# Issuing the low halves of weights one pair later, behind the next pair's sums and high halves

## The chip, the cores and the metric

The kernel runs on one core of a Trainium2 chip. Its engines work side by side, each through a queue of its own, in the order of the program: TensorE (PE) multiplies, VectorE (DVE) and ScalarE (ACT) work element by element, GpSimd (POOL) does a little, SyncE (SP) issues the transfers from the chip's memory. They wait for one another through semaphores. The metric is the time of one execution on the device, in microseconds (us); lower is better.

## The reference

The kernel computes one block of a streaming encoder on x of 256 positions by 2048 features, in fp32:

```python
x = x + 0.5 * swiglu(rms_norm(x), w_gate_1, w_up_1, w_down_1)
h = rms_norm(x);  P = h @ W_in
m = sigmoid(gate_gdn) * (gated_delta_net(P) @ W_A) + sigmoid(gate_att) * (chunk_attention(P) @ W_B)
x = x + m @ W_out
x = x + 0.5 * swiglu(rms_norm(x), w_gate_2, w_up_2, w_down_2)

def swiglu(h, w_gate, w_up, w_down):
    return (silu(h @ w_gate) * (h @ w_up)) @ w_down
```

The hidden width of the two feed-forward stages is 5504. Their weights, and those of the projections of the mixing stage between them, are read once from memory, and nearly all of the time goes into multiplying by them.

## The kernel before

**Numbers in two halves.** A product of fp32 accuracy is made of three matmuls on TensorE's fp32r format. Each operand is written as a high half (the value rounded to fp32r) and a low half (the value less its high half). `product` issues high by high (L359), high by low (L360) and low by high (L361) into one PSUM bank; the second operand is the weight.

**Weights come in pairs.** `plan` lists all weights in the order of use. `load` fetches one pair, two transfers of 512 KB on SP's queue (L283), into a raw buffer of 128x2x1024. `prepare` makes the halves. For a plain pair it does so piece by piece: ScalarE casts the high half (L113), VectorE subtracts it from the raw weight for the low half (L114), both 128x1024. Before it prepares a pair it sees that two more are loaded (LOAD = 2). `take_weights` hands the next weights out and prepares until more than PREP = 5 units stand ready (a piece is one unit, a fast pair four).

**Plain and fast pairs.** The gate and up products of a feed-forward stage run over 11 groups of 512 hidden columns (the last has 384), and in each group over 8 pairs j of 256 input features, with the gate weight and the up weight in one pair. Pairs 0, 2 and 5 (FAST) are fast, except in group 0 of the first stage: instead of 8 block products they use 7, on sums of blocks, in the manner of Winograd's scheme. That needs 24 matmuls for a plain pair and 21 for a fast one, 183 in a group. For a fast pair `prepare_sums` has VectorE make four sums S1 to S4 of weight blocks (L317 for two, L318, L319), has ScalarE cast the highs of the blocks that are used as they are (w and v, L325) and of the four sums (sh, 128x2048), and has VectorE subtract for the lows (L327), the last of them sl, 128x2048.

**A group.** `gate_up` goes through the 8 pairs and adds each product to one of 8 PSUM banks: four from the pool acc (results 1 to 4) and four from core (5 to 8). After the last fast pair it moves the banks of the fast products into four tiles e (L426 to L430). At the end of the group VectorE adds the four remaining banks, 2, 3, 4 and 8 (L439), ScalarE applies SiLU (L443), and VectorE multiplies gate by up (L446). A group's result is transposed on TensorE and split into halves (hid) a few pairs into the next group. Groups form chunks of 4, 4 and 3; behind each chunk the down product (pd) uses its hidden columns.

**The start.** In group 0 of the first stage, `feed(j)` brings x in: it scales and splits the block of x for pair j + 1 (L157, L158), issues the transfer of another block (L74), and from pair 3 on transposes x for the norm (`stand`). `finish` then takes the square root for the norm's factor rn, which the SiLU of the group needs.

**What sets the order.** Each engine's queue is the program's order as the scheduler lays it out from the order in which the Python code issues instructions. An instruction that waits holds everything behind it on its engine. The buffers of weights, their halves and the activations come from one heap of 22 slots.

**The mixing stage** multiplies by projections in the same way (pgt is one of its results). Near its middle GpSimd clears buffers (L818, L823) and copies blocks into them (L825, L826), which a small matmul of TensorE (pd, L858) waits for.

Of the kernel before, what the change touches and what calls it, by code (L numbers as in the profile page):

```python
# [12 lines left out]
F32R = mybir.dt.float32r  # L13
# [22 lines left out]
def block_kernel(ctx: ExitStack, tc: tile.TileContext, a: dict, out: bass.AP):  # L36
# [248 lines left out]
                nc.sync.dma_start(raw[:, at, : n * kk], src)  # L285
        loaded.append((i, fast, pieces, raw))

    def prepare():

        while len(loaded) < 1 + LOAD and len(loaded) < left[0]:  # L290
            load()
        left[0] -= 1
        i, fast, pieces, raw = loaded.popleft()
        if fast:
            return prepare_sums(i, pieces[0][1] * P, raw)
        for at, (src, n, kk) in enumerate(pieces):
            m = n * kk * (P if len(src.shape) == 3 else 1)
            w = heap([P, 2, 1024], F32R, f"w{i}{at}")
            hi, lo = w[:, 0, :m], w[:, 1, :m]
            split_to(hi, lo, raw[:, at, :m])  # L300
            if len(src.shape) == 3:
                n *= P
                cols = lambda w: [w.rearrange("p (c k x) -> p c k x", k=kk, x=P)[:, :, j, :] for j in range(kk)]
            else:
                cols = lambda w: [w[:, j * n : (j + 1) * n] for j in range(kk)]
            ready.append((1, (cols(hi), cols(lo), n)))

    def prepare_sums(i, n, raw):

        s = heap([P, 4, n], F32, f"s{i}")  # L310
        sh, sl = (heap([P, 4, n], F32R, f"s{x}{i}") for x in "hl")
        w1 = heap([P, 2, 2 * n], F32R, f"w{i}")
        w2 = heap([P, 2, n], F32R, f"v{i}")
        R = raw[:, :, : 2 * n].rearrange("p b (c k x) -> p b c k x", k=2, x=P)
        S = s.rearrange("p b (c x) -> p b c x", x=P)
        for b in range(2):
            nc.vector.tensor_sub(S[:, b], R[:, 1, :, b], R[:, b, :, 0])  # L317
        nc.vector.tensor_add(S[:, 2], S[:, 1], R[:, 0, :, 0])  # L318
        nc.vector.tensor_sub(S[:, 3], R[:, 0, :, 1], S[:, 2])  # L319
        col = lambda w: w.rearrange("p (c x) -> p c x", x=P)  # L320
        parts = (
            (w1[:, 0], w1[:, 1], raw[:, 0, : 2 * n]), (col(w2[:, 0]), col(w2[:, 1]), R[:, 1, :, 1]), (sh, sl, s),
        )
        for hi, lo, src in parts:
            nc.scalar.copy(hi, src)  # L325
        for hi, lo, src in parts:
            nc.vector.tensor_sub(lo, src, f32(hi))  # L327
        k = w1.rearrange("p s (c k x) -> p s c k x", k=2, x=P)
        w11, w21 = ([k[:, s, :, b, :] for s in range(2)] for b in range(2))
        t1, t3, t2, t4 = ((sh[:, b], sl[:, b]) for b in range(4))  # L330
        w22 = (w2[:, 0], w2[:, 1])

        ready.append((4, ((1, 0, w11), (2, 2, w21), (6, 5, t2), (7, 6, t3), (4, 3, t4), (5, 4, t1), (3, 7, w22))))

    left = [sum(1 for _ in plan())]

    def take_weights():
        tick()
        while sum(c for c, _ in ready) <= PREP and left[0]:
            prepare()  # L340
        return ready.popleft()[1]

    def run(gen):
# [42 lines left out]
    def gate_up(nm, f, i, xr, jobs, feed):  # L386
# [16 lines left out]
        ev = {}  # L403
        idle = 0
        for j in range(KD // 2):
            if feed:
                feed(j)
            if j in fast:
                ps = take_weights()
                for at, (b, i7, w) in enumerate(ps):  # L410
# [3 lines left out]
            else:  # L414
                for s in range(2):
                    wh, wl, _ = take_weights()
                    for k, w in enumerate(zip(wh, wl)):
                        for t in range(2):
                            add((2, 4, 3, 8)[2 * s + t], xr.st(2 * j + k, t), w)
                    idle += 1  # L420
                    if idle > 3 and jobs:
                        jobs.popleft()()
# [751 lines left out]
```

## Time and profile before

| | |
|---|---|
| median of 3 runs | 2180.31 us (2178.92 to 2181.02) |
| the profiled execution | 2180.59 us |
| its span, first to last instruction | 2178.8 us |
| TensorE busy | 2140.7 us, 98% of the span |
| VectorE busy | 1521.9 us, 70% |
| ScalarE busy | 1087.6 us, 50% |
| memory traffic | 434.61 MB, mean 199 GB/s |
| mean granted clock of TensorE | 0.998 of full speed |

The page's own share of the chain of work that ended last is PE 89%, DVE 5%, ACT 3%, issue 1%, DMA 1%. Busy time says how long an engine had work, not that the work was dense: matmuls overlap, one is recorded as 0.39 us long while the next starts 0.23 us after it. Where TensorE loses time is read from the distance of starts and from the waits, not from the busy share.

### The profile page before, as it was taken

The page shows a single profiled execution, that of the slowest core. Times are in us where ns is not written, and L with a number is a line of the kernel's source. Part 1 is how long each engine was busy: PE and PEld are TensorE (multiplying, and loading weights), DVE is VectorE, ACT ScalarE, POOL GpSimd, SP SyncE. Part 2 cuts the span into 40 slices and gives each one's busy share as a digit, 9 for nine tenths or more (in the row PEclk, how much of TensorE's full clock was granted, in tenths as well). Part 3 has the DMA queues.
Part 4 walks back from the last instruction along what each step waited for, and adds up shares of the span by engine and source line. Part 5 has one row for each costly group of instructions (what it writes and reads, how often), then busy time and mean ns, then how long its engine had stood idle before and what let it go on. Part 6 is the DMA issues. An engine that isn't in the chain of part 4 may idle for free.

```text
span 2178.8 us, 26078 instructions
## 1 busy us (share of the span) xinstructions
PE 2140.7 (98%) x9902; PEld 1776.1 (82%) x9902; DVE 1521.9 (70%) x1895; ACT 1087.6 (50%) x1318; POOL 8.3 (0%) x13
## 2 busy tenths in 40 slices
PE   7999999999999999999999999999999999999999
PEld 6777888788888988888878888887778887788887
DVE  6788587885867654666875645658886768857683
ACT  6555354553535544467645643545454435544351
POOL 0000000000000000000010000000000000000000
PEclk9999999999999999999999999999999999999999
DMA  9557765577647665445454556666568655686482
GB/s 302 190 179 226 241 208 181 182 239 234 213 146 252 247 215 195 156 134 176 160 174 155 176 191 201 197 210 199 189 192 255 222 191 174 205 258 214 155 265 83
DMA packets 397150, 434.61 MB, mean 199 GB/s; under 512 B 14672, under 2 KB 371296, under 8 KB 396768
## 3 DMA queue, kind: packets, MB, share of 16 engines
q1 hardware_dynamic: 397024, 432.95, 61.2%
q8 instruction: 77, 1.26, 0.2%
q14 instruction: 49, 0.40, 0.1%
HBM read 416.11 MB, written 16.79 MB: 199 GB/s over the span
## 4 chain that ended last, share of the span: by engine, by line
PE 89%; DVE 5%; ACT 3%; issue 1%; DMA 1%; POOL 0%; SPq 0%; ACTq 0%; DVEq 0%
PE pf L360 13%; PE pf L361 12%; PE pf L359 11%; PE pd L361 7%; PE pd L359 7%; PE pd L360 7%; DVE w L114 2%; PE pc L359 2%; PE pc L361 2%; PE pc L360 2%; PE pgt L359 2%; PE pgt L361 2%; PE pgt L360 2%; ACT w L113 2%; PE pwo L361 1%; PE pwo L360 1%
## 5 line engine op out<-in xcount | busy, mean ns | idle before, releaser
L114 DVE TENSOR_TENSOR w<-raw,w 128x1024 fp32r<-128x1024 f32 (+3 forms) x648 | 752.6, 1195 | 243.9 <-ACT w L113 239.4
L113 ACT CAST w<-raw 128x1024 fp32r<-128x1024 f32 (+3 forms) x648 | 640.4, 1031 | 292.4 <-PE pd L361 116.6
L359 PE MATMUL pf<-w,xr 128*128 128x512 f32 (+1 forms) x880 | 336.4, 388 | 5.7 <-ACT w L113 5.7
L360 PE MATMUL pf<-w,xr 128*128 128x512 f32 (+1 forms) x880 | 340.1, 386 | 1.9 <-DVE w L114 1.0
L361 PE MATMUL pf<-w,xr 128*128 128x512 f32 (+1 forms) x880 | 338.4, 385 | 0.0
L359 PE MATMUL pd<-w,hid 128*128 128x512 f32 x688 | 269.6, 392 | 0.0
L360 PE MATMUL pd<-w,hid 128*128 128x512 f32 x688 | 268.5, 390 | 0.0
L361 PE MATMUL pd<-w,hid 128*128 128x512 f32 x688 | 268.2, 390 | 0.0
L325 ACT CAST sh<-s 128x2048 fp32r<-128x2048 f32 (+1 forms) x63 | 117.7, 1868 | 265.9 <-DVE s L319 265.9
L327 DVE TENSOR_TENSOR sl<-s,sh 128x2048 fp32r<-128x2048 f32 (+1 forms) x63 | 141.1, 2239 | 88.0 <-ACT sh L325 88.0
L359 PEld LDWEIGHTS pf<-w,xr 128*128 128x128 f32 x880 | 164.1, 188 | 43.9 <-ACT w L113 13.9
L360 PEld LDWEIGHTS pf<-w,xr 128*128 128x128 f32 x880 | 165.3, 188 | 38.4 <-DVE w L114 7.6
L361 PEld LDWEIGHTS pf<-w,xr 128*128 128x128 f32 x880 | 165.3, 188 | 30.7
L361 PEld LDWEIGHTS pd<-w,hid 128*128 128x128 f32 x688 | 129.2, 188 | 26.7
L359 PEld LDWEIGHTS pd<-w,hid 128*128 128x128 f32 x688 | 129.2, 188 | 26.6
L360 PEld LDWEIGHTS pd<-w,hid 128*128 128x128 f32 x688 | 129.3, 188 | 26.4
L359 PE MATMUL pgt<-w,xr 128*128 128x512 f32 x256 | 102.0, 398 | 0.0
L360 PE MATMUL pf<-sl,xf 128*128 128x512 f32 (+1 forms) x252 | 99.3, 395 | 2.4 <-DVE sl L327 2.4
L361 PE MATMUL pgt<-w,xr 128*128 128x512 f32 x256 | 100.8, 394 | 0.0
L360 PE MATMUL pgt<-w,xr 128*128 128x512 f32 x256 | 100.6, 393 | 0.0
L361 PE MATMUL pf<-sh,xf 128*128 128x512 f32 (+1 forms) x252 | 97.0, 387 | 0.0
L359 PE MATMUL pf<-sh,xf 128*128 128x512 f32 (+1 forms) x252 | 88.7, 396 | 5.3 <-ACT sh L325 5.3
(324 smaller groups left out, 3214.8 us busy)
## 6 DMA issues: line engine op xcount, KB each, us to landing
raw<-wd SPq DMA_DIRECT2D x168, 512.0 KB, 5.1
raw<-wg SPq DMA_DIRECT2D x160, 512.0 KB, 3.7
raw<-wu SPq DMA_DIRECT2D x160, 512.0 KB, 4.8
raw<-wgt SPq DMA_DIRECT2D x64, 512.0 KB, 4.6
raw<-wa SPq DMA_DIRECT2D x48, 512.0 KB, 4.6
raw<-wc SPq DMA_DIRECT2D x48, 512.0 KB, 4.2
raw<-wbr SPq DMA_DIRECT2D x32, 512.0 KB, 4.4
raw<-wo SPq DMA_DIRECT2D x32, 512.0 KB, 5.9
```

What stands on the lines that cost most here:

```text
L113: nc.scalar.copy(hi, src)
L114: nc.vector.tensor_sub(lo, src, f32(hi))
L325: nc.scalar.copy(hi, src)
L327: nc.vector.tensor_sub(lo, src, f32(hi))
L359: nc.tensor.matmul(dst, ah, wh, start=start, stop=False)
L360: nc.tensor.matmul(dst, ah, wl, start=False, stop=False)
L361: nc.tensor.matmul(dst, al, wh, start=False, stop=stop)
```

## The change

`prepare_sums` and the old `prepare` become one function `begin` for the first part of a pair: the loads behind it, the sums (two of the four now in one operation of 128x1024), and all casts of high halves. What is left to do, the subtractions for low halves, goes on a list with the weights (`begun`). `prepare` then issues a pair's lows only after the next pair's `begin`. At the very first `take_weights` nothing stands ready, no next pair is begun, and the loop stops as soon as one pair is prepared (min(PREP, taken[0])). `feed(j)` is called behind the first `take_weights` of the pair and no longer ahead of it.

```diff
--- before.py
+++ after.py
@@ -285,59 +285,75 @@
                 nc.sync.dma_start(raw[:, at, : n * kk], src)
         loaded.append((i, fast, pieces, raw))
 
-    def prepare():
+    def begin():
+
 
         while len(loaded) < 1 + LOAD and len(loaded) < left[0]:
             load()
         left[0] -= 1
         i, fast, pieces, raw = loaded.popleft()
-        if fast:
-            return prepare_sums(i, pieces[0][1] * P, raw)
-        for at, (src, n, kk) in enumerate(pieces):
-            m = n * kk * (P if len(src.shape) == 3 else 1)
-            w = heap([P, 2, 1024], F32R, f"w{i}{at}")
-            hi, lo = w[:, 0, :m], w[:, 1, :m]
-            split_to(hi, lo, raw[:, at, :m])
-            if len(src.shape) == 3:
-                n *= P
-                cols = lambda w: [w.rearrange("p (c k x) -> p c k x", k=kk, x=P)[:, :, j, :] for j in range(kk)]
-            else:
-                cols = lambda w: [w[:, j * n : (j + 1) * n] for j in range(kk)]
-            ready.append((1, (cols(hi), cols(lo), n)))
-
-    def prepare_sums(i, n, raw):
-
+        if not fast:
+            todo, out = [], []
+            for at, (src, n, kk) in enumerate(pieces):
+                m = n * kk * (P if len(src.shape) == 3 else 1)
+                w = heap([P, 2, 1024], F32R, f"w{i}{at}")
+                hi, lo = w[:, 0, :m], w[:, 1, :m]
+                nc.scalar.copy(hi, raw[:, at, :m])
+                todo.append((hi, lo, raw[:, at, :m]))
+                if len(src.shape) == 3:
+                    n *= P
+                    cols = [w[:, s, :m].rearrange("p (c k x) -> p c k x", k=kk, x=P) for s in range(2)]
+                    cols = [[w[:, :, j, :] for j in range(kk)] for w in cols]
+                else:
+                    cols = [[w[:, s, j * n : (j + 1) * n] for j in range(kk)] for s in range(2)]
+                out.append((1, (*cols, n)))
+            begun.append((todo, out))
+            return
+        n = pieces[0][1] * P
         s = heap([P, 4, n], F32, f"s{i}")
-        sh, sl = (heap([P, 4, n], F32R, f"s{x}{i}") for x in "hl")
         w1 = heap([P, 2, 2 * n], F32R, f"w{i}")
         w2 = heap([P, 2, n], F32R, f"v{i}")
         R = raw[:, :, : 2 * n].rearrange("p b (c k x) -> p b c k x", k=2, x=P)
         S = s.rearrange("p b (c x) -> p b c x", x=P)
-        for b in range(2):
-            nc.vector.tensor_sub(S[:, b], R[:, 1, :, b], R[:, b, :, 0])
+        nc.vector.tensor_sub(S[:, 0:2], R[:, 1].rearrange("p c k x -> p k c x"), R[:, :, :, 0])
         nc.vector.tensor_add(S[:, 2], S[:, 1], R[:, 0, :, 0])
         nc.vector.tensor_sub(S[:, 3], R[:, 0, :, 1], S[:, 2])
         col = lambda w: w.rearrange("p (c x) -> p c x", x=P)
-        parts = (
-            (w1[:, 0], w1[:, 1], raw[:, 0, : 2 * n]), (col(w2[:, 0]), col(w2[:, 1]), R[:, 1, :, 1]), (sh, sl, s),
-        )
+        parts = [(w1[:, 0], w1[:, 1], raw[:, 0, : 2 * n]), (col(w2[:, 0]), col(w2[:, 1]), R[:, 1, :, 1])]
         for hi, lo, src in parts:
             nc.scalar.copy(hi, src)
-        for hi, lo, src in parts:
-            nc.vector.tensor_sub(lo, src, f32(hi))
+        sh, sl = (heap([P, 4, n], F32R, f"s{x}{i}") for x in "hl")
+        nc.scalar.copy(sh, s)
+        parts.append((sh, sl, s))
         k = w1.rearrange("p s (c k x) -> p s c k x", k=2, x=P)
         w11, w21 = ([k[:, s, :, b, :] for s in range(2)] for b in range(2))
         t1, t3, t2, t4 = ((sh[:, b], sl[:, b]) for b in range(4))
         w22 = (w2[:, 0], w2[:, 1])
 
-        ready.append((4, ((1, 0, w11), (2, 2, w21), (6, 5, t2), (7, 6, t3), (4, 3, t4), (5, 4, t1), (3, 7, w22))))
+        prods = ((1, 0, w11), (2, 2, w21), (6, 5, t2), (7, 6, t3), (4, 3, t4), (5, 4, t1), (3, 7, w22))
+        begun.append((parts, [(4, prods)]))
+
+    begun = deque()
+    taken = [0]
+
+    def prepare():
+
+        if not begun or (taken[0] and left[0]):
+            begin()
+        if len(begun) == 1 and taken[0] and left[0]:
+            begin()
+        todo, out = begun.popleft()
+        for hi, lo, src in todo:
+            nc.vector.tensor_sub(lo, src, f32(hi))
+        ready.extend(out)
 
     left = [sum(1 for _ in plan())]
 
     def take_weights():
         tick()
-        while sum(c for c, _ in ready) <= PREP and left[0]:
+        while sum(c for c, _ in ready) <= min(PREP, taken[0]) and (left[0] or begun):
             prepare()
+        taken[0] += 1
         return ready.popleft()[1]
 
     def run(gen):
@@ -403,8 +419,6 @@
         ev = {}
         idle = 0
         for j in range(KD // 2):
-            if feed:
-                feed(j)
             if j in fast:
                 ps = take_weights()
                 for at, (b, i7, w) in enumerate(ps):
@@ -414,6 +428,8 @@
             else:
                 for s in range(2):
                     wh, wl, _ = take_weights()
+                    if feed and s == 0:
+                        feed(j)
                     for k, w in enumerate(zip(wh, wl)):
                         for t in range(2):
                             add((2, 4, 3, 8)[2 * s + t], xr.st(2 * j + k, t), w)
```

The scheduler turns this into another order on each engine. ScalarE at the start, from its first scaling of x on (raw_95 and raw_98 are the first two pairs' raw buffers, xf_0 and xr_1 the blocks of x for pairs 0 and 1):

```order
L157 ACTIVATE xf_0_102<-xT_80,vec 128x256 x2
L157 ACTIVATE xr_1_109<-xT_80,vec 128x256 x2
L113 CAST w_118<-raw_95 128x1024
L113 CAST w_121<-raw_95 128x1024
L157 ACTIVATE xr_1_109<-xT_80,vec 128x256 x2
L113 CAST w_127<-raw_98 128x1024
L113 CAST w_130<-raw_98 128x1024
```

The same place in the changed kernel:

```order
L157 ACTIVATE xf_0_102<-xT_80,vec 128x256 x2
L301 CAST w_112<-raw_95 128x1024
L301 CAST w_114<-raw_95 128x1024
L157 ACTIVATE xr_1_118<-xT_80,vec 128x256 x2
L301 CAST w_141<-raw_98 128x1024
L301 CAST w_143<-raw_98 128x1024
L301 CAST w_148<-raw_109 128x1024
```

The cast of the first weights now stands ahead of the scaling of the second block of x.

SyncE's queue at the same place (raw_98 is the second raw pair, xT are blocks of x). Before:

```order
L283 DMA raw_98<-wg 128x4x256
L283 DMA raw_98<-wu 128x4x256
L74 DMA xT_80<-x 128x512 x3
L1005 DMA cst<-cst 128x768
L283 DMA raw_115<-wg 128x4x256
L283 DMA raw_115<-wu 128x4x256
L283 DMA raw_124<-wg 128x4x256
L283 DMA raw_124<-wu 128x4x256
```

And in the changed kernel, right behind the second raw pair:

```order
L74 DMA xT_80<-x 128x512
L283 DMA raw_109<-wg 128x4x256
L283 DMA raw_109<-wu 128x4x256
L74 DMA xT_80<-x 128x512
L283 DMA raw_138<-wg 128x4x256
L283 DMA raw_138<-wu 128x4x256
L283 DMA raw_145<-wg 128x4x256
L283 DMA raw_145<-wu 128x4x256
L283 DMA raw_168<-wg 128x4x256
L283 DMA raw_168<-wu 128x4x256
L74 DMA xT_80<-x 128x512
L1021 DMA cst<-cst 128x768
```

Before, three transfers of x and the constants stand between the second raw pair (raw_98) and the third (raw_115). Now one transfer of x stands there, another behind the third raw pair, and the third, with the constants, behind the sixth (raw_168).

VectorE where the third group of the first stage begins (names with 4 in e_4 belong to the second group; sl_818 and sl_820 are the low sums of the third group's fast pair 0). Before:

```order
L317 TENSOR_TENSOR s_816<-raw_753 128x512 x2
L327 TENSOR_TENSOR w_819<-raw_753,w_819 128x1024
L318 TENSOR_TENSOR s_816<-s_816,raw_753 128x512
L327 TENSOR_TENSOR v_820<-raw_753,v_820 128x512
L319 TENSOR_TENSOR s_816<-raw_753,s_816 128x512
L439 TENSOR_TENSOR e_4_0_795<-pf_4_2_579,e_4_0_795 128x512
L439 TENSOR_TENSOR e_4_1_796<-pf_4_3_599,e_4_1_796 128x512
L439 TENSOR_TENSOR e_4_2_797<-pf_4_4_591,e_4_2_797 128x512
L439 TENSOR_TENSOR e_4_3_798<-pf_4_8_645,e_4_3_798 128x512
L327 TENSOR_TENSOR sl_818<-s_816,sh_817 128x2048
L114 TENSOR_TENSOR w_870<-raw_804,w_870 128x1024
L114 TENSOR_TENSOR w_873<-raw_804,w_873 128x1024
```

And in the changed kernel:

```order
L320 TENSOR_TENSOR s_811<-raw_697,s_811 128x512
L347 TENSOR_TENSOR v_813<-raw_697,v_813 128x512
L455 TENSOR_TENSOR e_4_0_799<-pf_4_2_592,e_4_0_799 128x512
L455 TENSOR_TENSOR e_4_2_801<-pf_4_4_604,e_4_2_801 128x512
L347 TENSOR_TENSOR sl_820<-s_811,sh_819 128x2048
L318 TENSOR_TENSOR s_873<-raw_808 128x1024
L347 TENSOR_TENSOR w_827<-raw_757,w_827 128x1024
L319 TENSOR_TENSOR s_873<-s_873,raw_808 128x512
L347 TENSOR_TENSOR w_829<-raw_757,w_829 128x1024
L320 TENSOR_TENSOR s_873<-raw_808,s_873 128x512
L455 TENSOR_TENSOR e_4_1_800<-pf_4_3_612,e_4_1_800 128x512
L455 TENSOR_TENSOR e_4_3_802<-pf_4_8_650,e_4_3_802 128x512
```

Before, all four additions of banks stand ahead of the low sums. Now the additions of banks 2 and 4 do, and those of 3 and 8 stand behind the low sums, behind the next fast pair's four sums (s_873) and the two lows of the plain pair between (w_827, w_829).

TensorE in that same fast pair 0, from the sixth of its matmuls on (sh and sl are the halves of the sums, w and v those of the blocks used as they are; line numbers of the changed kernel are 16 higher). Before:

```order
L361 MATMUL pf_8_2_901<-w_819,xf_0_102 128x512
L359 MATMUL pf_8_6_905<-sh_817,xf_0_102 128x512
L359 MATMUL pf_8_7_909<-sh_817,xf_0_102 128x512
L359 MATMUL pf_8_4_913<-sh_817,xf_0_102 128x512
L359 MATMUL pf_8_5_917<-sh_817,xf_0_102 128x512
L359 MATMUL pf_8_3_921<-v_820,xf_0_102 128x512
L360 MATMUL pf_8_3_921<-v_820,xf_0_102 128x512
L361 MATMUL pf_8_3_921<-v_820,xf_0_102 128x512
L359 MATMUL pf_8_2_901<-w_870,xr_1_109 128x512
L360 MATMUL pf_8_6_905<-sl_818,xf_0_102 128x512
L361 MATMUL pf_8_6_905<-sh_817,xf_0_102 128x512
L360 MATMUL pf_8_7_909<-sl_818,xf_0_102 128x512
```

And in the changed kernel:

```order
L377 MATMUL pf_8_2_911<-w_812,xf_0_102 128x512
L375 MATMUL pf_8_6_915<-sh_819,xf_0_102 128x512
L376 MATMUL pf_8_6_915<-sl_820,xf_0_102 128x512
L377 MATMUL pf_8_6_915<-sh_819,xf_0_102 128x512
L375 MATMUL pf_8_7_919<-sh_819,xf_0_102 128x512
L376 MATMUL pf_8_7_919<-sl_820,xf_0_102 128x512
L377 MATMUL pf_8_7_919<-sh_819,xf_0_102 128x512
L375 MATMUL pf_8_4_923<-sh_819,xf_0_102 128x512
L376 MATMUL pf_8_4_923<-sl_820,xf_0_102 128x512
```

The high sums are first used by the 7th matmul of the pair in both kernels. The low sums were first used by the 15th, and now are by the 8th.

## Rows read from the trace of the kernel before

**Rows 1.** The page, part 1: busy time of each engine over the span.
```profile
PE 2140.7 (98%) x9902; PEld 1776.1 (82%) x9902; DVE 1521.9 (70%) x1895; ACT 1087.6 (50%) x1318; POOL 8.3 (0%) x13
```

**Rows 2.** The view of waits, TensorE only: tile and line that waited, engine, tile and line waited for; us in total, times, longest.
```profile
PE pf L359 <- ACT w L113: 19.9, 14, 14.2
PE pf L359 <- ACT sh L325: 5.3, 11, 1.1
PE pd L858 <- POOL gdn_pk L826: 2.7, 1, 2.7
PE pf L360 <- DVE sl L327: 2.4, 9, 0.8
PE pf L359 <- ACT g L443: 1.2, 1, 1.2
PE pf L360 <- DVE w L114: 1.0, 6, 0.2
```

**Rows 3.** Windows from the first use of a fast pair's low sums to the same place one group later, in a chunk of each of the two feed-forward stages; columns: window, length, then busy time (instructions) of PE, PEld, DVE, ACT, POOL, granted TensorE clock, DMA share, GB/s.
```profile
113.15:158.22 45.07, 43.94 (x192) 34.72 (x192) 38.34 (x44) 22.46 (x25) 0.00 (x0) 1.00 0.58 187
...
1815.18:1860.23 45.05, 44.07 (x191) 34.64 (x191) 38.34 (x44) 22.48 (x25) 0.00 (x0) 1.00 0.58 187
```

**Rows 4.** The timeline of TensorE in the first of these groups; columns: start, length, engine, line, operation, output<-inputs, shape, count, and in brackets the idle time before and its releaser.
```profile
115.34 0.39 PE L361 MATMUL pf<-w,xr 128*128 128x512 f32 x1
...
120.10 0.39 PE L361 MATMUL pf<-w,xr 128*128 128x512 f32 x1
...
122.14 0.39 PE L361 MATMUL pf<-v,xf 128*128 128x512 f32 x1
122.89 1.20 PE L359 MATMUL pf<-sh,xf 128*128 128x512 f32 x4 [0.36 <-ACT sh L325]
...
124.78 0.73 PE L359 MATMUL pf<-w,xr 128*128 128x512 f32 x2 [0.45 <-ACT w L113]
125.35 0.39 PE L360 MATMUL pf<-sl,xf 128*128 128x512 f32 x1
...
140.13 0.39 PE L359 MATMUL pf<-sh,xf 128*128 128x512 f32 x1
...
142.09 0.40 PE L360 MATMUL pf<-sl,xf 128*128 128x512 f32 x1
```

**Rows 5.** The timeline of VectorE and ScalarE around the first two fast pairs of that group (pair 0 starts on TensorE at 109.49, pair 2 at 120.33).
```profile
109.01 1.89 DVE L439 TENSOR_TENSOR e<-pf,e 128x512 f32<-128x512 f32 x3 [0.20 <-PE pf L361]
110.82 2.28 DVE L327 TENSOR_TENSOR sl<-s,sh 128x2048 fp32r<-128x2048 f32 x1
...
120.93 1.91 ACT L325 CAST sh<-s 128x2048 fp32r<-128x2048 f32 x1 [6.12 <-DVE s L319]
...
122.87 2.29 DVE L327 TENSOR_TENSOR sl<-s,sh 128x2048 fp32r<-128x2048 f32 x1 [2.03 <-ACT sh L325]
```

**Rows 6.** The timeline of the first 19 us, all engines, and the time of the first weight transfer from issue to landing.
```profile
1.65 0.43 SPq L283 DMA_DIRECT2D raw<-wg  x1
...
12.27 0.91 ACT L157 ACTIVATE xr<-xT,vec 128x256 fp32r<-128x256 f32 x2 [6.47 <-DMA xT<-x]
13.08 1.98 ACT L113 CAST w<-raw 128x1024 fp32r<-128x1024 f32 x2
...
14.16 1.22 PE L359 MATMUL pf<-w,xf 128*128 128x512 f32 x2 [14.16 <-ACT w L113]
...
18.56 0.39 PE L359 MATMUL pf<-w,xf 128*128 128x512 f32 x1
```

**Rows 7.** The view of one line's instructions (the weight transfers, L283), for the one issued at 1.65: time from issue to landing.
```profile
DMA to landing us min/median/max: 4.7/4.7/4.7
```

**Rows 8.** The timeline where the first group of the first stage ends and the second begins.
```profile
71.05 0.69 ACT L443 ACTIVATE g<-pf,rn 128x512 f32<-128x512 f32 x1
...
71.79 0.50 PE L359 MATMUL pf<-w,xf 128*128 128x512 f32 x1 [1.24 <-ACT g L443]
```

**Rows 9.** The timeline of the mixing stage at the one place where TensorE waits there, and windows over the same place (columns as in rows 3).
```profile
1119.73 1.81 POOL L818 MEMSET gdn_T<- 128x2048 f32 x1 [1119.29 <-DVE w L114]
...
1123.77 0.39 PE L361 MATMUL pgt<-w,xr 128*128 128x512 f32 x1
...
1126.84 2.71 PE L858 MATMUL pd<-gdn_ls,gdn_pk 128*128 128x32 f32 x16 [2.68 <-POOL gdn_pk L826]
...
1129.37 0.77 PE L359 MATMUL pgt<-w,xr 128*128 128x512 f32 x1
...
1126.80:1129.40 2.60, 2.56 (x17) 2.56 (x17) 0.00 (x0) 2.55 (x5) 1.21 (x2) 0.71 0.00 0
1129.40:1135.00 5.60, 5.60 (x15) 4.40 (x16) 2.36 (x2) 1.43 (x4) 0.00 (x0) 0.53 0.35 109
```

**Rows 10.** VectorE's instructions grouped by line and shape: count, busy us, mean ns, and idle time before them.
```profile
L114 DVE TENSOR_TENSOR w<-raw,w 128x1024 fp32r<-128x1024 f32 x598 | 710.3, 1220 | 237.8 <-ACT w L113 233.8 <-DMA x<-xd 1.5 <-DMA raw<-wd 0.5
L327 DVE TENSOR_TENSOR sl<-s,sh 128x2048 fp32r<-128x2048 f32 x57 | 130.5, 2290 | 81.6 <-ACT sh L325 81.6
L317 DVE TENSOR_TENSOR s<-raw 128x512 f32<-128x512 f32 x114 | 73.4, 683 | 0.0
```

## The prediction

> **What bounds the kernel now.** I read the busy times first: TensorE is busy 98% of the span, VectorE 70%, ScalarE 50% [rows 1]. TensorE sets the end, and since the number of its matmuls doesn't change, only its waits can be won. So the second view is that of TensorE's waits alone [rows 2]: it waits for the first cast at the start (14.2 us), and 38 more times in the gate and up products, for highs (ACT w: 13 times, 5.7 us without the first), high sums (11, 5.3), low sums (8, 1.6 without the longest, 0.8, which belongs to the start) and lows (6, 1.0). Of other kinds there are two that matter: one for SiLU (1.2) and one for GpSimd in the mixing stage (2.7).
>
> Third, what such waits really cost. Matmuls start 4.76 us apart over 21 of them, or 0.2267 each [rows 4]. A group has 183 and 8 transposes. Between 140.13 and 142.09 stand 4 matmuls and 8 transposes, so these add 1.96 - 4 x 0.2267 = 1.05. A group without waits takes 41.49 + 1.05 = 42.54 us; the windows show 45.07 and 45.05 [rows 3]. A steady group therefore loses 2.5 us, of which the listed idle is only about 0.20 + 0.36 + 0.45 + 0.17 = 1.2: the wait at 122.89 is listed as 0.36, but its start is 0.52 later than the spacing allows, and the matmuls behind it start late too (124.78, two of them, to 125.35: 0.12 more) [rows 4].
>
> Fourth, why the halves come late. Low sums of pair 0 run at 110.82 to 113.1 because the additions of three banks, among them the last of the old group, stand ahead of them (109.01); in pair 2 VectorE idles 2.03 us until ScalarE has cast the high sums, and ScalarE had idled 6.12 us for the last sum [rows 5]. The sums are issued too late, not too slowly.
>
> **The change part by part.** *Sums and highs earlier.* In the changed order pair 0's sums and casts of highs are issued ahead of the lows of the pair before. Let T be the start of pair 0 on TensorE. The low sums of pair 0 now have only the additions of banks 2 and 4 ahead. The last matmul of bank 4 is the 13th before T, so issued at T - 2.95 and over some 0.4 later; an addition of 0.68 and the low sums of 2.29 [rows 10] end at about T + 0.4. TensorE asks for them with the 8th matmul, T + 1.59: a margin of 1.2 us, where it now waits. Behind them stand four sums, two lows, the additions of banks 3 and 8, two multiplications by the gate and two lows, then the low sums of pair 2: with 1.13 us for 128x1024 and 0.60 for 128x512 from start to start (a little less than the lengths of 1.22 and 0.68 [rows 10]) these are about 8.9 us, and the low sums end near T + 11.5. They are wanted 56 matmuls after T, at T + 12.7; margin again 1.2. Bank 3's addition ends near T + 5.7, and its successor is wanted at T + 6.8 (30 matmuls). Pair 5 has over 4 us. All listed waits of a steady group go on paper. What is late next is the same low sums, 1.2 us below the surface.
>
> The sum: 8 steady groups (8 waits for low sums [rows 2]) at 2.5 are 20 us. The 13.6 us of listed idle, less 8 x 1.2, leave 4.0 for the other groups; with what restarts add, at least 0.3 for each of some 8 waits, that is 6 to 9, and I take 7. Of 27 I leave 2 as small rests: **25 us**. The bounds are 0 (if the margins are gone) and 29.
>
> *Two sums in one.* 57 times 2 x 0.683 become one of the size of a low, 1.22: 0.147 x 57 = 8 us of VectorE [rows 10]. VectorE doesn't bound (38.3 of 45 us in a steady group [rows 3]), so it counts nothing itself. A gain of 0.15 us in each margin is in the walk above. Reading two blocks with another stride in one operation isn't in the trace; if it went at half speed it would cost 1.2 us each, just the margin: bounds 0 and, at worst, 57 x 1.2 = 68, of which I count nothing: the single sums read such blocks already and take 0.683 for 512 columns, in step with 1.22 for the 1024 of a low that reads in order [rows 10].
>
> *The start.* Now the cast of the first weight stands behind the scaling of the second block of x, which waits for its transfer until 12.27; the cast starts at 13.08 and TensorE at 14.16 [rows 6]. The first weight was there long before: issued at 1.65, landed 4.7 us later, 6.4 [rows 6, 7]. With the cast ahead, TensorE starts at 6.4 + 1.05, near 7.5: 6.7 us earlier. Some is given back at once, since pair 4's block of x now stands behind two more raw pairs: about 1 us; the last pair would start some 6 us earlier than before. But at the end of this group SiLU needs the norm's factor, and TensorE the bank that SiLU empties: it waits for it until 71.79 [rows 8]. That chain, transposes of x, squares, square root, two table loads and the casts in between, is no shorter, and the next pair's casts now stand inside it. Adding it up over ScalarE's queue in the new order I get SiLU done near 66.8, 5.0 earlier, with TensorE 6 matmuls less far (1.4): **3.6 us**. Bounds: 1.5 (the chain moves only by what TensorE's transposes move less a cast of 1.9 and its waits) and 6.5 (the whole lead).
>
> *The mixing stage.* GpSimd's clearing starts at 1119.73 behind a low, and TensorE waits for its copies until 1126.84: starts 1123.77 and 1126.84 are 3.07 apart, so 2.84 are lost. [...] In the new order that small matmul stands 14 matmuls (3.2 us) later, and the low that GpSimd waits for is a little later too, by about 1.3. The wait falls from 2.8 to about 1.0: 1.8 us gained for sure if the rest holds, up to 5.5 if the clock stays. I take **3.5**. [...]
>
> Counted at nothing: the loads, since a slot of the heap is released long before (two pairs, about 10 us of TensorE's work, stand loaded in both kernels); the down products and projections, where TensorE does not wait [rows 2].
>
> Sum: 25 + 3.6 + 3.5 = 32.1. The profiled execution is 2180.6 (span 2178.8 and 1.8 around it), 0.3 above the median: 2180.6 - 32.1 - 0.3 = **2148 us**.
>
> **The rivals.** *All is kept* (chance 0.13): the start's whole 6.1, groups 29, mixing 5.5, together 40.6: 2140. For it: the chain at 71.79 may be shorter than I add up. Against: the casts in it.
>
> *Half is kept* (0.15): margins of 1.2 us are hand sums over ten instructions; if low sums come as late as TensorE asks in every second place, 13 of 25 stay, with 1.5 from the start and 1.8 from mixing: 2164. For it: idle VectorE time in a group is under 7 us [rows 3], and each wait of an engine's queue moves what is behind.
>
> *The lows are not the cause* (0.06): the sums and highs wait on buffers that come free only with TensorE's use of the pair before, so they run as late as now, only issued earlier. Then only start and mixing gain: about 2174. Against it: ScalarE idled 6.12 us for a sum, not for a buffer [rows 5].
>
> *Slower* (0.04): TensorE's new order relies on the low sums (8th matmul in pair 0 instead of the 15th). If they end as late as now, at 3.6 us into pair 0 and 4.8 into pair 2 (122.87 + 2.29 against 120.33) [rows 5], the waits are 2.0 and 2.3, with two restarts 4.9 in place of 2.5 a group: 8 x 2.4 = 19 more, less 7 at start and mixing: 2193. It decides from low sums 1.6 us into the pair on. The mechanism would be VectorE's queue: sums that wait for a transfer hold up the lows behind them. [...]
>
> **How the numbers follow.** The forecast has 0.62 and its own range 2143 to 2156. The range 2139 to 2167 takes in most of the first two rivals and leaves out the rest and half of the ends: about 2 in 10. A measurement of this kernel tells a change from none at about 0.2%, 4.4 us. Faster than that: 0.62 + 0.13 + 0.15 and half of the third rival, 0.93; no change 0.03; slower 0.04.
>
> **What would show it.** Right: the first matmul near 7.5; TensorE's waits for high sums and low sums gone from steady groups, and their windows at 42.5 to 43; the wait for SiLU ended near 67; the wait for GpSimd at about 1 us. Wrong: waits of 1 us or more for low sums in pair 0 or 2, a group longer than 44 us, sums on VectorE that wait for raw weights, or a merged sum far from 1.22 us.

## The result and the profile after

The changed kernel takes 2148.84 us (median of 4 runs, 2148.53 to 2149.85) against 2179.83 for the kernel before (median of 4, 2178.92 to 2181.02), a ratio of 0.9858 with a 95% interval of 0.9841 to 0.9875. The forecast was 2148. The sum was right; two of its terms and one of its reasons were not.

The view of TensorE's waits has only these left above 0.4 us in the changed kernel (columns as in [rows 2]):

```profile
PE pf L375 <- ACT w L301: 7.2, 1, 7.2
PE pd L874 <- POOL gdn_pk L842: 3.9, 1, 3.9
PE pf L375 <- ACT g L459: 2.8, 1, 2.8
PE pf L375 <- ACT xr L157: 0.8, 1, 0.8
```

The 38 waits of the gate and up products for highs, high sums, low sums and lows are gone; what stands under "ACT w" is the first matmul alone (7.2 us where it was 14.2). The wait for GpSimd is longer, 3.9 us for 2.7. A steady group (the third or fourth of a chunk of four), from the start of pair 0 to the next, as a window (columns as in [rows 3]):

```profile
106.59:149.41 42.82, 42.79 (x193) 34.98 (x191) 38.24 (x41) 22.76 (x26) 0.00 (x0) 1.00 0.61 197
```

It takes 42.82 us for 45.07, with VectorE as busy as before. It is the slowest of the eight: the other seven take 42.55 to 42.59 us, where they took 45.04 to 45.15. As windows, such a group in the second chunk, then the short last group of the first stage (384 columns), each before and after:

```profile
372.19:417.31 45.12, 43.94 (x193) 34.70 (x191) 38.34 (x44) 22.51 (x25) 0.00 (x0) 1.00 0.57 187
364.04:406.63 42.59, 42.59 (x193) 35.05 (x191) 38.07 (x41) 22.52 (x25) 0.00 (x0) 1.00 0.61 197
634.96:670.28 35.32, 33.79 (x193) 32.35 (x191) 30.13 (x40) 20.11 (x27) 0.00 (x0) 1.00 0.82 259
621.21:654.01 32.80, 32.80 (x193) 32.47 (x192) 29.34 (x38) 18.01 (x24) 0.00 (x0) 1.00 0.91 287
```

The timeline of VectorE, and one row of ScalarE, in the group from 106.59 on (pair 0 starts at 106.59, pair 2 at 116.79), to be read beside [rows 5]:

```profile
103.39 1.37 DVE L455 TENSOR_TENSOR e<-pf,e 128x512 f32<-128x512 f32 x2
104.78 2.29 DVE L347 TENSOR_TENSOR sl<-s,sh 128x2048 fp32r<-128x2048 f32 x1
...
111.60 1.28 DVE L455 TENSOR_TENSOR e<-pf,e 128x512 f32<-128x512 f32 x2
...
115.86 2.28 DVE L347 TENSOR_TENSOR sl<-s,sh 128x2048 fp32r<-128x2048 f32 x1
...
111.78 1.92 ACT L326 CAST sh<-s 128x2048 fp32r<-128x2048 f32 x1 [2.44 <-DVE s L320]
```

And TensorE's first matmul with the low sums of pair 0:

```profile
108.17 0.39 PE L376 MATMUL pf<-sl,xf 128*128 128x512 f32 x1
```

The low sums of pair 0 run to 107.07 and are used at 108.17: a margin of 1.1 us. Over all steady groups the margin in pairs 0 and 2 is 0.97 to 1.25.

The start and the end of the first group, to be read beside [rows 6, 8]:

```profile
6.14 1.04 ACT L301 CAST w<-raw 128x1024 fp32r<-128x1024 f32 x1 [0.49 <-DMA raw<-wg]
7.24 1.22 PE L375 MATMUL pf<-w,xf 128*128 128x512 f32 x2 [7.24 <-ACT w L301]
...
65.61 0.69 ACT L459 ACTIVATE g<-pf,rn 128x512 f32<-128x512 f32 x1
66.34 0.50 PE L375 MATMUL pf<-w,xf 128*128 128x512 f32 x1 [2.79 <-ACT g L459]
```

The mixing stage, to be read beside [rows 9]:

```profile
1107.69 1.81 POOL L834 MEMSET gdn_T<- 128x2048 f32 x1 [1107.26 <-DMA raw<-wgt]
...
1114.81 3.34 PE L874 MATMUL pd<-gdn_ls,gdn_pk 128*128 128x32 f32 x16 [3.90 <-POOL gdn_pk L842]
```

The first matmul of the products pgt around it, before and after, from which the moments of this stage are counted below:

```profile
1072.32 0.39 PE L359 MATMUL pgt<-w,xr 128*128 128x512 f32 x1
1055.89 0.39 PE L375 MATMUL pgt<-w,xr 128*128 128x512 f32 x1
```

And as windows behind that wait (columns as before, the clock third from the end):

```profile
1114.80:1117.40 2.60, 2.59 (x14) 2.60 (x14) 0.00 (x0) 1.54 (x3) 1.21 (x2) 0.57 0.03 10
1117.40:1123.00 5.60, 5.60 (x22) 4.68 (x22) 1.22 (x1) 2.02 (x3) 0.00 (x0) 0.59 0.00 0
```

The memset's row names a DMA as its releaser, but the transfer is not what its start fits: VectorE's low before it, at 1106.42 for 1.22 us, ends at 1107.64, and the memset starts at 1107.69.

Where the 32.0 us went (span 2178.8 to 2146.8) is seen from the first starts on TensorE of each kind of product, gate and up (pf) and down (pd). A stage is the time from the first to the next kind; the first column is the moment of the first down product:

| kernel | first pd at | second chunk, stage 1 | third | mixing with its last pd | first chunk, stage 2 | second | third |
|---|---|---|---|---|---|---|---|
| before | 199.69 | 174.73 | 119.82 | 790.01 | 178.73 | 174.66 | 119.80 |
| changed | 192.00 | 169.19 | 116.84 | 791.05 | 170.38 | 169.16 | 116.86 |

The five later chunks give 5.54 + 2.98 + 8.35 + 5.50 + 2.94 = 25.3. Of the 7.7 us up to the first down product, 4.8 belong to two steady groups (2.25 and 2.54), so 2.9 are left for the start: the third group of the first stage starts at 106.59 for 109.49. The mixing stage loses 1.0.

### The profile page after: what moved, and what is told of

The parts are those of the page before. It is cut to its first block, busy times and chain, and to the rows that moved or that the text cites. A ratio compares the mean times of both kernels' runs of the same rounds, so it can differ in the third digit from the quotient of the medians.

```text
span 2146.8 us, 26104 instructions
## 1 busy us (share of the span) xinstructions
PE 2127.0 (99%) x9902; PEld 1780.9 (83%) x9902; DVE 1521.4 (71%) x1832; ACT 1091.9 (51%) x1318; POOL 8.3 (0%) x13
## 4 chain that ended last, share of the span: by engine, by line
PE 96%; SPq 1%; DVE 1%; DMA 1%; issue 1%; ACT 1%; POOL 0%; POOLq 0%; ACTq 0%
PE pf L376 13%; PE pf L377 13%; PE pf L375 13%; PE pd L377 7%; PE pd L376 7%; PE pd L375 7%; PE pgt L377 2%; PE pgt L375 2%; PE pgt L376 2%; PE pc L375 2%; PE pc L377 2%; PE pc L376 2%; PE pwo L376 1%; PE pwo L375 1%; PE pwo L377 1%; PE hid L123 1%
## 5 line engine op out<-in xcount | busy, mean ns | idle before, releaser
L347 DVE TENSOR_TENSOR w<-raw,w 128x1024 fp32r<-128x1024 f32 (+3 forms) x711 | 834.0, 1195 | 304.5 <-ACT w L301 299.6
L377 PEld LDWEIGHTS pd<-w,hid 128*128 128x128 f32 x688 | 129.1, 188 | 26.9
L377 PE MATMUL pf<-sh,xf 128*128 128x512 f32 (+1 forms) x252 | 97.2, 386 | 0.0
L324 ACT CAST w<-raw 128x1024 fp32r<-128x1024 f32 (+1 forms) x63 | 65.0, 1031 | 61.3 <-PE pf L377 24.7
```

The lines of the kernel that those rows point to most:

```text
L377: nc.tensor.matmul(dst, al, wh, start=False, stop=stop)
```

## Experiments

Each was timed in at least three rounds beside the kernel before on the same chip. The kernel before took 2179.47 to 2180.27 us (medians) in these.

**Two sums in two operations again.** In the changed kernel:

```diff
-nc.vector.tensor_sub(S[:, 0:2], R[:, 1].rearrange("p c k x -> p k c x"), R[:, :, :, 0])
+for b in range(2):
+    nc.vector.tensor_sub(S[:, b], R[:, 1, :, b], R[:, b, :, 0])
```

> The changed kernel with the first two sums in two operations again. Order theory (sums and highs ahead of the lows make the gain): VectorE has 1.2 us of margin at each fast pair and loses 0.15 there, so 2149 to 2151, no waits for sums or lows on TensorE. Rival (the shorter sum makes a good part of it): the waits for high sums come back, 2155 to 2165.

Measured: 2149.92 us, ratio to before 0.9865 (0.985 to 0.988); no wait for sums or lows. It can't be told from the changed kernel's 0.9858.

**The merged sum alone,** the same edit the other way in the kernel before.

> The kernel before with nothing but the two sums in one operation. Order theory: the sums end 0.15 us earlier, at most two waits in each steady group shrink by that, 16 x 0.15 = 2.4 us: 2177 to 2180. Rival: 2160 to 2170.

Measured: 2178.17 us, 0.9995 (0.9985 to 1.0004): no change that can be told, and on TensorE the waits for high sums fell from 5.3 to 3.6 us while those for low sums rose from 2.4 to 3.0. The merged sum is worth nothing here by itself.

**The start alone,** in the kernel before:

```diff
-    while sum(c for c, _ in ready) <= PREP and left[0]:
+    while sum(c for c, _ in ready) <= min(PREP, taken[0]) and left[0]:
         prepare()
+    taken[0] += 1
...
-            if feed:
-                feed(j)
...
                     wh, wl, _ = take_weights()
+                    if feed and s == 0:
+                        feed(j)
```

> The kernel before with the start of the change alone (only one pair prepared at first, feed behind the first take, so the loads in the new order). The trace after shows the first stage 7.7 us shorter, of which some 5 belong to its two steady groups, so the start is worth 2.7: 2176 to 2178, the first matmul near 7.3, steady groups still 45.1 us. Rival (the earlier start is lost in the wait for SiLU): 2179 to 2181.

Measured: 2176.30 us, 0.9986 (0.9977 to 0.9996). First matmul at 7.36. The first down product comes at 195.06, 4.6 earlier than before; of the 6.8 us at the first matmul some went into the next groups. The longest waits rose there, as the view of TensorE's waits shows:

```profile
PE pf L361 <- ACT sh L325: 6.8, 12, 1.3
PE pf L362 <- DVE sl L327: 2.9, 9, 1.4
```

**The change without its start** (two pairs prepared at first, feed ahead of the take; the edit above undone in the changed kernel).

> The changed kernel with the start as before (two pairs prepared at first, feed ahead of the take). If the parts add up, 2148.8 + 2.7 = 2151 to 2153 with groups of 42.6 us. Rival (the start costs nothing in the end): 2148 to 2149.

Measured: 2155.40 us, 0.9891 (0.9875 to 0.9908), first down product at 198.74 for 192.00. The parts don't add up to 2151 to 2153: the start is worth 6.6 us in the new order and 3.2 in the old one. TensorE waits for SiLU until

```profile
73.38 0.50 PE L375 MATMUL pf<-w,xf 128*128 128x512 f32 x1 [2.38 <-ACT g L459]
```

where the changed kernel waits until 66.34 and the kernel before until 71.79 [rows 8]. Without the start, ScalarE's chain behind the first group ends later than before: its first squaring for the norm starts at 58.70 for 57.76, and from there to SiLU's start it takes 13.94 us for 13.29, with one more cast in it (v, 0.60). Why the start gives back more than that is not shown. In the split of the 32.0 us above it has 2.9, given the order.

**Only the sums ahead.** Highs are cast with a pair's own lows again, sums and loads stay a pair ahead:

```diff
 def prepare():
...
+    for hi, lo, src in todo:
+        nc.scalar.copy(hi, src)
     for hi, lo, src in todo:
         nc.vector.tensor_sub(lo, src, f32(hi))
```

(and the three casts in begin left out)

> The changed kernel, but only a pair's sums (and the loads) go ahead of the lows of the pair before; its highs are cast with its own lows, as in the kernel before. Theory that the late sums are the cause (ScalarE waited 6 us for a sum, VectorE 2 us for the highs of sums): all or nearly all of the gain stays, 2148 to 2153. Rival (ScalarE's casts of highs must also be a pair early): waits for sh and w on TensorE come back, 2160 or more.

Measured: 2177.19 us, 0.9988 (0.9978 to 0.9997). Nearly all the gain is lost, and with it the theory as I had put it, that sums ahead would keep it. The waits for high and low sums did go, but others took their place. TensorE's waits:

```profile
PE pf L373 <- DVE e L453: 10.9, 10, 1.3
PE pf L373 <- ACT w L343: 8.7, 3, 7.6
PE pd L872 <- POOL gdn_pk L840: 5.4, 1, 5.4
```

And in the timeline the place of the largest:

```profile
114.60 1.88 DVE L453 TENSOR_TENSOR e<-pf,e 128x512 f32<-128x512 f32 x3
115.33 0.50 PE L373 MATMUL pf<-sh,xf 128*128 128x512 f32 x1 [1.06 <-DVE e L453]
```

Three additions of banks now stand behind the next pair's sums and two lows, and TensorE waits for a bank. A group takes 44.72 us (108.60 to 153.32). The time lies where this run's rival has it, but not by its mechanism: waits for sh did not come back, and those for w only twice beyond the first (1.1 us in all). It is nearer the mechanism of the prediction's rival *Slower*: work put ahead in VectorE's queue holds what stands behind it, here bank additions rather than lows (the ten waits for e, 10.9 us).

**Only the plain highs ahead,** that is all but those of the sums (w and v of a fast pair go ahead too). The sums and the cast of their highs go with a pair's own lows:

```diff
-nc.vector.tensor_sub(S[:, 0:2], R[:, 1].rearrange("p c k x -> p k c x"), R[:, :, :, 0])
...
-nc.scalar.copy(sh, s)
+def sums():
+    nc.vector.tensor_sub(S[:, 0:2], R[:, 1].rearrange("p c k x -> p k c x"), R[:, :, :, 0])
...
+    nc.scalar.copy(sh, s)
...
-todo, out = begun.popleft()
+todo, out, sums = begun.popleft()
+if sums:
+    sums()
```

> The changed kernel, but only the plain highs (and the loads) go a pair ahead; the four sums and the cast of their highs are issued with the pair's lows, as before. Theory that the late sums are the cause: the waits for high sums and low sums in the groups stay, and of the 24 us that the order alone gave (2155.4 against 2179.5) most is lost: 2168 to 2176 with the start's gain. Rival: 2149 to 2158.

Measured: 2151.76 us, 0.9873 (0.9859 to 0.9888). This was the wrong way round too: with the sums where they were, all but 3 us of the gain stays. The timeline of ScalarE before and in this kernel, around the high sums of pair 2 of the third group, shows what differs. First the kernel before, behind the cast of the high sums at 120.93 [rows 5]:

```profile
122.74 3.89 ACT L113 CAST w<-raw 128x1024 fp32r<-128x1024 f32 x4
```

And here, with VectorE's last sum (pair 2 starts on TensorE at 117.14):

```profile
110.71 2.00 ACT L301 CAST w<-raw 128x1024 fp32r<-128x1024 f32 x2
116.55 0.68 DVE L328 TENSOR_TENSOR s<-raw,s 128x512 f32<-128x512 f32 x1
117.32 1.91 ACT L329 CAST sh<-s 128x2048 fp32r<-128x2048 f32 x1 [4.62 <-PE pf L382]
119.14 1.04 ACT L301 CAST w<-raw 128x1024 fp32r<-128x1024 f32 x1
```

Before, the cast of the high sums waits 6.12 us at the head of ScalarE's queue, and four casts of plain highs stand behind it; TensorE meets the first of these at 123.92 and waits for the second until 124.78 [rows 4]. Here two casts of plain highs (110.71) are done before the cast of the sums begins to wait, and those behind it belong to later pairs. The cast of the sums still waits for the last sum: its row names TensorE, but it starts 0.09 us after that sum's end (116.55 + 0.68), as it did before (120.16 + 0.68, and 120.93). TensorE, too, has something to do: its order now has matmuls of the next plain pair, whose highs are ready, ahead of those with high sums. The scheduler lays out another order of TensorE in each of these kernels. In pair 0 the low sums are first used by the 20th matmul here, where it was the 15th before; in pair 2 by the 23rd, where it was the 17th. No run keeps TensorE's order and moves only the casts, so what the early highs give by themselves and what they give through this order is not told apart.

**The plain highs ahead and nothing else** (sums in two operations, the start as before).

> The kernel before with the plain highs (and loads) a pair ahead and nothing else: sums in two operations, with the pair's own lows, the start as before. If the highs held behind the waiting cast of high sums are the cause and the parts add up: 2151.8 + 6.5 for the start + 1.1 for the two operations = 2159, between 2157 and 2161, no waits for ACT w or sh in steady groups. Rival (the highs need the merged sum or the new start beside them): 2165 or more.

Measured: 2156.39 us, 0.9894 (0.9877 to 0.991): no wait for ACT w or sh in the groups, and 2.6 us less than the parts added up to, 0.6 below the range given. It needs neither the merged sum nor the start.

**Only the plain pairs' highs ahead,** those of a fast pair with its sums.

> The changed kernel with only the plain pairs' highs ahead; a fast pair's sums and highs are issued with its lows. If it is the plain highs, stuck on ScalarE behind the cast of high sums, that TensorE lacked: as with all plain highs ahead, 2151 to 2155. Rival (the fast pair's own highs w and v must be early, since its lows on VectorE stand between the sums): 2160 or more.

Measured: 2155.20 us, 0.9887 (0.9872 to 0.9902), 0.2 above what was expected. The second and third chunks are within 0.3 us of those with all plain highs ahead (169.56, 116.78, 169.56, 116.78 us); most of the loss is in the first chunk, whose down product comes at 196.62 for 192.38. The profiled execution was the slowest of the four (2157.47), so a part of that is its own. The fast pairs' own highs need not be early.

**Everything a pair earlier, in the old order.** One number in the kernel before:

```diff
-PREP, LOAD = 5, 2
+PREP, LOAD = 7, 2
```

> The kernel before with PREP 7 for 5: everything of a pair (sums, highs, lows) is issued earlier, the order within and between pairs stays. Theory of the held queue (ScalarE's cast of high sums waits for a late sum and holds the next pair's plain highs behind it): the order is what counts, and TensorE still meets them late or not according to how much lead the extra units give; a gain of some 10 us, 2165 to 2172. Theory that the halves were simply prepared too late: nearly the whole gain, 2155 to 2160. Theory that only the new order helps: 2178 to 2180.

Measured: 2153.38 us, 0.9882 (0.9867 to 0.9897). That is the theory of halves prepared too late, and 2 us better than it said; the theory that the order counts fell. The old order gives a group of 42.77 us (42.75 to 42.93 in the other steady ones), and no wait of its groups is left. The window of a group:

```profile
109.59:152.36 42.77, 42.77 (x193) 34.98 (x192) 38.27 (x44) 22.46 (x25) 0.00 (x0) 1.00 0.60 196
```

and of TensorE's waits those above 2 us:

```profile
PE pf L359 <- ACT w L113: 13.6, 1, 13.6
PE pd L858 <- POOL gdn_pk L826: 3.9, 1, 3.9
```

The order inside the queues is one way to make the highs early; more lead is another, and does as much (2153.38 us, beside 2155.40 for the change without its start).

**One operation more on VectorE in each fast pair** (the low of w is computed twice, ahead of the low sums).

```diff
+parts.insert(0, parts[0])
 parts.append((sh, sl, s))
```

> The changed kernel with one more VectorE operation of 1.13 us in each fast pair (the low of w is computed twice), ahead of the low sums. The prediction gave the low sums a margin of 1.2 us: with that, 2149 to 2152 and no or hardly any wait for sl on TensorE. Rival (the margin is used up, VectorE's order sets the group): two waits of some 1 us in each of some 16 groups, 2165 to 2185.

Measured: 2148.15 us, 0.9857 (0.9843 to 0.9872): 0.85 below what was expected, nothing lost, no wait for low sums. The window of a steady group shows VectorE's work filling up and the group no longer:

```profile
105.50:148.08 42.58, 42.58 (x193) 35.06 (x191) 41.20 (x44) 22.51 (x25) 0.00 (x0) 1.00 0.59 197
```

In pair 0 the low sums end at 106.85 and are first used at 107.09, so 0.24 of the margin is left. In pair 2 they end 13.55 us into the group, later than the 12.7 at which the changed kernel uses them; here TensorE's order uses them later, at 13.85. For pair 2 this run is therefore no measure of the old margin.

**The mixing stage in the old order,** its pairs not begun ahead:

```diff
-if not begun or (taken[0] and left[0]):
+if not begun:
     begin()
-if len(begun) == 1 and taken[0] and left[0]:
+if len(begun) == 1 and taken[0] and left[0] and not MIX[0] <= begun[0][2] < MIX[1]:
     begin()
```

> The changed kernel with the old order for the pairs of the mixing stage alone (lows right behind the highs of the same pair). The wait of TensorE for GpSimd in the mixing stage rose from 2.7 to 3.9 us. If the later lows hold GpSimd's clearing back, it falls to 2.7 and the time by about 1 us: 2147 to 2148.5. Rival (the wait comes from how the feed-forward stage hands over, or from the shared slots): stays 3.9, 2148.8.

Measured: 2147.86 us, 0.9852 (0.9837 to 0.9866); the wait is back at 2.7 us and the stage at 790.14. What did it is not that lows are issued later, though. GpSimd's first memset, counted from the start of the products pgt around it, starts 47.4 us in before (1119.73 - 1072.32) and here, and 51.8 us in the changed kernel (1107.69 - 1055.89), in the two with all plain highs ahead but not the sums, and with PREP 7, where the lows are earlier and not later; with the sums alone ahead it is 50.6. It goes with pairs being begun earlier. With PREP 7, too, the memset (1111.55) starts right behind the end of a low (1110.27 and 1.22 long). That this is the low of a later pair than before, since the memset's slot of the heap has then been through one more pair's hands, is my reading and not shown.

**GpSimd's clearing and copies issued earlier** in the changed kernel, at the 17th of the 31 steps of the loop ahead of them:

```diff
 for j in range(B32 - 1):
...
+    if j == 16:
+        Tt = heap([P, 2 * H, P], F32, "gdn_T")
+        nc.gpsimd.memset(Tt, 0.0)
...
```

> The changed kernel with GpSimd's three clearings and its copies issued some 15 steps earlier in the mixing stage, so that their buffers are claimed earlier. If the wait of 3.9 us and the half clock behind it come from the clearing alone: both go, 4.1 us of wait and 2 to 3 us of slow matmuls, 2141 to 2144. Rival (VectorE's transposes and ScalarE's copies into the same buffers end as late): 2146 to 2149.

Measured: 2142.93 us, 0.9828 (0.9814 to 0.9843), 5.9 us less than the changed kernel and the fastest version of all. The memset starts at 1089.51, the wait is gone, and so is the lower clock, as the timeline and then windows over the place show:

```profile
1089.51 1.81 POOL L831 MEMSET gdn_T<- 128x2048 f32 x1 [1089.07 <-DVE w L347]
```

```profile
1095.00:1105.00 10.00, 10.00 (x45) 7.97 (x44) 9.80 (x12) 8.97 (x12) 2.70 (x6) 1.00 0.63 211
1105.00:1115.00 10.00, 9.88 (x52) 8.09 (x51) 8.41 (x9) 6.74 (x9) 0.00 (x0) 1.00 0.60 191
1115.00:1125.00 10.00, 10.00 (x54) 8.55 (x53) 6.94 (x9) 5.09 (x8) 0.00 (x0) 1.00 0.72 230
```

The mixing stage falls by 6.4 us (791.05 to 784.61): 3.9 are listed wait, and the other 2.5 I put down to the lower clock and restarts, so the stall of TensorE cost here about 1.6 times its length.

## Why the prediction was right, and where not

*The bound.* Right: TensorE's waits were all there was to win, and those of the groups went.

*The size of the groups' term.* It was 25 us and measured 25.3 + 4.8 = 30.1. The steady groups were sized right: eight at 2.5 made 20, and they gave 2.25 to 2.58 each, 20.0 together; a group without waits was to take 42.54, and seven of the eight take 42.55 to 42.59. The other groups gave 10.1 where I took 7, and nothing was lost to the small rests for which I left 2. I had sized these groups from listed idle alone, 0.3 to a wait. The two short last groups gave 2.5 each, as much as a steady one (35.32 to 32.80 and 35.31 to 32.83), the first group of the second stage 2.65 (45.35 to 42.70), and five second groups of a chunk some 0.5 each. I should have measured them from first to last start, as the steady groups.

*The margins* were right: the low sums of pair 0 end at T + 0.48 (said T + 0.4), those of pair 2 start at T + 9.27 and with 2.28 end at T + 11.55 (said 11.5), and bank 3's addition starts at T + 5.0 and is over, at 0.68, by T + 5.7 (said 5.7). The doubled low, which leaves 0.24 of it in pair 0 and costs nothing, says that a margin of some 1.1 us is there.

*The reason.* Wrong in part. "The sums are issued too late" was read from ScalarE's 6.12 and VectorE's 2.03 us of idle [rows 5]. Sums ahead do take the waits for sums away, but alone they push three bank additions back in the order that the scheduler made of them, and TensorE waits for a bank instead. Plain highs ahead take the same waits away at a small part of that price (two waits for a bank, 1.4 us, where there were ten, 10.9), with the sums as late as before: ScalarE's idle ahead of the sums is still there and costs nothing, because in TensorE's new order another pair's matmuls stand in its place. A pair's lead for everything, in the old order, does as much. So what is shown is that the lead of the highs, with the order of TensorE that the scheduler makes of it, is enough and the place of the sums is not needed; whether sums ahead with the bank additions kept in place would be enough too stays open, since no run tried it. Loads are a pair earlier in the sums-only version as well, and did not save it.

*The merged sum* was rightly counted at nothing, from both sides. Half speed for strided blocks did not come: the operation takes 1.21 to 1.22 us.

*The start.* 3.6 us said, 2.9 found. The wait for SiLU ended at 66.34 (said 66.8), and TensorE had come 6 matmuls less far, as said. What the sum left out is the lower granted clock behind that wait (0.70 over 66.30 to 72.00), 1.6 us (last section). But 2.9 is a figure for this sum only: taken out of the changed kernel the start costs 6.6.

*The mixing stage* is the step that failed: 3.5 us were to be gained and 1.0 was lost. The small matmul did come 3.2 us later (TensorE was free 51.84 us after the start of pgt before, 1126.84 - 2.68 - 1072.32, and 55.02 after), but GpSimd's memset came 4.4 us later, not 1.3, so the wait grew by 1.2. I had followed the instruction that it waited for in the old trace through the new order, and not asked what else moves with it. No run shows the term of 3.5, nor the 5.5 that I had put above it as the stall's full price for a wait of 2.8: both were my estimates, from that wait and the slower matmuls behind it. In the trace of the kernel before, the 13 spacings from 1129.37 [rows 9] to 1134.90 are 0.43 us on the mean, together 2.6 more than at 0.2267, with the granted clock at 0.53:

```profile
1129.94 0.63 PE L360 MATMUL pgt<-w,xr 128*128 128x512 f32 x1
1130.37 0.63 PE L361 MATMUL pgt<-w,xr 128*128 128x512 f32 x1
...
1134.90 0.39 PE L360 MATMUL pgt<-w,xr 128*128 128x512 f32 x1
```

What the runs showed in their place is 6.4 us for a wait of 3.9, by the early clearing, and a granted clock of 0.57 and 0.59 behind that wait in the changed kernel, 1.00 where the early clearing leaves no wait. So the term came out with the other sign, 4.5 us from the forecast, and the part that the clock was to give back was lost with it.

*The rivals.* None came. That the total is within 1 us of the forecast is luck: a groups' term 5.1 too small stands against a mixing term 4.5 and a start 0.7 too large. The 20 us of the steady groups are not luck.

## What to carry to other kernels

When an engine's queue idles in front of one instruction, ask first who needs that instruction and who needs those behind it: the late one may cost nothing if the consumer has other work that is ready. Before rewriting an order, try the plain lead: preparing one pair more in the old order gave 26.9 of the 31.0 us. A stall outside the path that a change speaks of can move with it (here 2.7 us became 3.9); look at what claims its buffers, and issue that earlier.

## What the runs showed of the hardware that was not expected

Two waits of TensorE in the changed kernel cost more than their length, with a lower granted clock and wider spacing of matmuls behind them. That for GpSimd (3.90 us, then a clock of 0.57 and 0.59) is one. The other is that for SiLU (2.79 us, until 66.34); windows behind it, and one in the kernel with the doubled low, where two waits of 1.92 and 1.27 us with work between them stand at this place instead. The changed kernel:

```profile
66.30:72.00 5.70, 5.66 (x18) 4.50 (x19) 5.68 (x6) 4.01 (x5) 0.00 (x0) 0.70 0.62 188
72.00:80.00 8.00, 8.00 (x37) 6.63 (x36) 7.45 (x8) 5.21 (x5) 0.00 (x0) 1.00 0.72 225
```

and with the doubled low:

```profile
64.00:70.00 6.00, 4.73 (x22) 3.56 (x21) 5.33 (x11) 5.97 (x8) 0.00 (x0) 1.00 0.15 48
```

Behind the longer wait the granted clock was 0.70 on the mean of the window, and eight matmuls in a row started 0.43 us apart, 1.6 us lost; behind the two shorter ones it stayed at 1.00. In the profiled executions the version with more work takes 46.35 us for its second group, where the changed kernel takes 47.95, which fits that loss, and comes to its first down product at 190.64 for 192.00. The whole times, 2148.15 and 2148.84, can't be told apart.

In these runs the length of a wait does not decide it alone. With only the plain highs ahead, waits of 1.30 and 1.95 us stand at this place, with nine matmuls between them where the doubled low has twelve, and behind the second the granted clock was 0.70 as well:

```profile
65.90:71.60 5.70, 5.64 (x18) 4.52 (x19) 5.57 (x7) 2.04 (x4) 0.00 (x0) 0.70 0.27 85
```

What decides between the two cases is not shown.

VectorE's 41.20 us of work in a group of 42.58, 97%, in the kernel with the doubled low made TensorE wait nowhere in that group.
